# A four-layer diffusion-transformer step: the first gate and up pair by plain block products, and two bursts of the modulation product in other places

## The chip, the cores and the metric

The kernel runs on one core of one Trainium2 chip. The time is the device time of one execution in microseconds (us), from the first to the last instruction with what lies around them; lower is better. TensorE (PE) does the matrix products, VectorE (DVE) and ScalarE (ACT) the elementwise work, GpSimd (POOL) some of it, and SyncE (SP) issues nearly all transfers.

## The reference

Four layers, each with its own token mixer, run over 640 tokens (512 latent, 128 context) with D = 1024 and a feed-forward width of 2816. All data are float32. What matters here:

```python
for li in range(DEPTH):
    mp = adaln(c_ctx[None, :], w_mod[li], b_mod[li])      # silu(c) @ w_mod + b_mod, 6 vectors of D
    ms = adaln(c, w_mod[li], b_mod[li])
    ...                                                   # mixer: op, os_ (with the output product w_o)
    xp = xp + mp[2] * op
    xs = xs + ms[2] * os_
    xp = xp + mp[5] * swiglu(modulate(rms_norm(xp, norm2_g[li]), mp[3], mp[4]), ffn_w_gate[li], ffn_w_up[li], ffn_w_down[li])
    xs = xs + ms[5] * swiglu(modulate(rms_norm(xs, norm2_g[li]), ms[3], ms[4]), ffn_w_gate[li], ffn_w_up[li], ffn_w_down[li])
# swiglu(h) = (silu(h @ w_gate) * (h @ w_up)) @ w_down
```

## The kernel before

Activations lie transposed: 8 feature blocks of 128 partitions by 640 tokens, and a matrix product works on the token halves 0..319 and 320..639. A float32 product is made of three products of split operands (high by high, high by low, low by high; tiles `hh`, `hl` of the activations and `whi`, `wlo` of the weights). A weight block comes in as `raw` by a transfer that SP issues; ACT casts it to `whi`, and DVE subtracts to get `wlo` (both in `two`).

`rest(L)` is the second part of layer L: the second half of the output product w_o, the residual, the RMS norm's statistics, gate and up, and down. `halves_first` runs the output product; for its last two feature blocks it does token half 0 of both blocks, then token half 1 (24 products each). `stat` squares x on ACT (L494), sums on DVE (`t`, L496) and lets TensorE add over the partitions (the matmuls `big<-t,consts`); ACT makes `rstd` of the result (L505, L512).

Gate and up are 2 x 11 matrices, each of 256 output features by 1024 inputs, numbered m = 0..21 (gate and up in turn; a gate with its up is a pair). Each is computed by the Strassen-Winograd scheme: 7 block products in place of 8 for a 2 x 2 split of weights (A11..A22, output halves by input halves) and activations (B11..B22, input halves by token halves). A block product is 12 matmuls of 128 x 128 by 128 x 320 (4 blocks of 128 inputs, three products each). The scheme needs the sums S1..S4 of the weights (`make_a`, DVE, L695, then cast and split as a weight is) and T1..T4 of the activations (`make_b`), and result sums on DVE (`sv`, L719 and below). `make_b` multiplies by `rstd` (DVE, L656), makes the high part on ACT and the low part on DVE (L649) for B11 and B21 tile by tile, then the T tiles, and B22 last.

The modulation of layer L+1 is computed meanwhile: a **burst** is a transfer of 4 x 512 KB (`rawm`, L455, in `mod_load`) and 16 matmuls (`sm<-rawm,cond`; the trace has 32 rows for them); after every second burst ACT copies the result out (`modev`), and 4 small matmuls (`sm<-consts,modev`) and DVE add it up. `rawm` has room for one burst, so the transfer of a burst waits for the matmuls of the one before. `fill(n)` puts n bursts in at its place in the program; layers 0 to 2 have such bursts, layer 3 has none.

The order on each engine is set by a scheduler that takes the instructions by their priority in the program, except where `issue_after` ties one to another. Each engine goes through its own list in order, and so does SP's queue of transfers. There are 4 slots for `raw`, 9 each for `whi` and `wlo`, 4 for `sum`, and 6 PSUM banks named `big`.

Of the kernel before, what the change touches and what calls it, by code (L numbers as in the profile page):

```python
# [8 lines left out]
F32 = mybir.dt.float32  # L9
F32R = mybir.dt.float32r  # L10
AF = mybir.ActivationFunctionType
ALU = mybir.AluOpType
# [250 lines left out]
class Net:  # L263
# [6 lines left out]
    def mm(self, out, lhsT, rhs, start, stop):  # L270
        return self.nc.tensor.matmul(out, lhsT=lhsT, rhs=rhs, start=start, stop=stop, skip_group_check=True)  # L271
# [205 lines left out]

    def flush(self):
        while self.filler:
            self.fill(1)  # L480
# [144 lines left out]
    def make_b(self, pool, L, B, raws):  # L625
# [36 lines left out]
        for i in range(HALF):  # L662
            for d in (i, i + HALF):
                raw(d, hi)
                p, m = raws[d][:, NL:], more[:, d:d + 1]
                nc.scalar.activation(p, p, AF.Identity, bias=m)
            a, b, t = raws[i], raws[i + HALF], t3[i // 2][:, i % 2]
            self.sub(nc.vector, t, b[:, hi], a[:, hi])
            self.sub(nc.vector, a[:, hi], a[:, hi], a[:, lo])
            two("T1", i, hi, a[:, hi])  # L670
# [9 lines left out]
        for i in range(HALF):  # L680
            two("22", i + HALF, hi, raws[i + HALF][:, hi], shift[:, i + HALF, 0:1])
# [16 lines left out]
    def block(self, out, A, B, start, stop):  # L698

        h, l = self.two(A, self.nc.vector)  # L700
        for k, (xh, xl) in enumerate(B):
# [3 lines left out]
            self.mm(out, l[:, c], xh, False, stop and k == len(B) - 1)  # L705

    def gate_up(self, fp, L, name, i, B, pair):
# [32 lines left out]
        if i == 0:  # L740
            self.block(d, A["S1"], B["T1"], True, True)
        self.block(b, A["S2"], B["T2"], True, True)
        add(v1, b, s1)
        if i:
            self.block(d, A["S1"], B["T1"], True, True)
# [8 lines left out]
        if up:  # L754
            for r in (1, 0):
                hi, lo = (fp.tile([P, T], F32R, tag="a", name=n, bufs=16) for n in ("ah", "al"))
                nc.scalar.copy(hi, pair[r])
                self.sub(nc.vector, lo, pair[r], hi.bitcast(F32))
                pair[r] = (hi, lo)
# [39 lines left out]
    def rest(self, L):  # L799

        nc, tc, a = self.nc, self.tc, self.a
        with tc.tile_pool(name=f"ffn{L}", bufs=1, reuse_waits="tile") as fp:
            self.slots(fp)
            todo = 0
            if L + 1 < self.depth:
                c0 = self.mod_done.get(L + 1, 0)
                todo = (6144 - c0) // (4 * MODW) * (ND // BURST) + 1 - 2 * EDGE
                self.filler = [self.mod_parts(L + 1, c0, 6144, fp)]
            B, raws = {}, {}
# [11 lines left out]
            self.fill(EDGE)  # L821
# [9 lines left out]
            ahead(0)  # L831
            ahead(1)
            next(gens[0])
            next(gens[1])
            next(B_steps)
            for part, (i0, i1) in enumerate(PAIRS):
                if part:
                    ahead(2 * i0)
                for m in range(2 * i0, 2 * i1):
                    if m > 1:  # L840
                        next(gens[m])
                    next(gens[m])
                    if 0 < m < 2 * i1 - 1:
                        ahead(m + 1)
                    next(gens[m])
# [909 lines left out]
```

## Time and profile before

| | |
|---|---|
| runs (median of 3; lowest to highest) | 3220.17 us (3213.5 to 3220.33) |
| the profiled execution's own time | 3216.05 us |
| its span, first to last instruction | 3214.0 us |
| mean granted TensorE clock | 0.976 of full speed |
| TensorE busy, of the span | 94% |
| VectorE / ScalarE / GpSimd busy | 67% / 48% / 19% |

The profiled execution takes 2.05 us beside its span and lies 4.1 us under the median of the runs. TensorE is busy for nearly the whole span, but the granted clock is below full speed in places, and there a matmul counts as busy for longer; and busy shares are means over stages with different limits.

### The profile page before, as it was taken

How to read it: one execution, taken by the hardware profiler on the slowest of the kernel's cores; microseconds unless marked ns; L12 is line 12 of the kernel's file. 1: busy time of each engine (PE TensorE's matmuls, PEld its weight loads, DVE VectorE, ACT ScalarE, POOL GpSimd, SP SyncE). 2: the span in 40 equal slices, each digit the busy share in tenths (PEclk: the TensorE clock that was granted, in tenths of full speed). 3: DMA queues.
4: the chain of work that ended last, by engine and by line, in shares of the span. 5: the costliest groups of instructions: out<-in, count | busy, mean ns of one | idle time of the engine just before them, and what ended most of it. 6: DMA issues, size and time to landing. Idle time of an engine off the chain costs nothing.

```text
span 3214.0 us, 57273 instructions
## 1 busy us (share of the span) xinstructions
PE 3029.7 (94%) x21901; PEld 2841.6 (88%) x21901; DVE 2161.6 (67%) x4522; ACT 1528.5 (48%) x3264; POOL 607.1 (19%) x691
## 2 busy tenths in 40 slices
PE   7998989999999989999986899899999999899999
PEld 6997879999988779999985778899998878799999
DVE  5555587666586768585768766867575775875765
ACT  4555454333356755242446664434243576543432
POOL 2553200000044420000025542000001553100000
PEclk9998999999999999999998999999999999899999
DMA  8346563232433342222211224522233111132322
GB/s 265 97 123 208 176 224 102 70 92 94 147 102 128 112 155 76 83 83 76 87 53 37 63 75 143 170 89 80 83 132 118 52 32 32 53 99 70 96 66 86
DMA packets 159027, 331.41 MB, mean 103 GB/s; under 512 B 18592, under 2 KB 40480, under 8 KB 158752
## 3 DMA queue, kind: packets, MB, share of 16 engines
q1 hardware_dynamic: 155584, 323.46, 32.3%
q8 instruction: 173, 2.83, 0.4%
q10 hardware_dynamic: 3168, 4.28, 0.4%
q14 instruction: 102, 0.84, 0.1%
HBM read 303.86 MB, written 4.28 MB: 96 GB/s over the span
## 4 chain that ended last, share of the span: by engine, by line
PE 81%; DVE 8%; DMA 5%; ACT 3%; issue 1%; POOL 1%; SPq 0%; DVEq 0%; ACTq 0%; POOLq 0%
PE big L271 53%; PE sm L271 18%; PE S L271 6%; PE tp L1009 3%; DMA rawm<-in_wmod 3%; DMA k<-k 1%; PE tp L271 1%; DMA raw<-in_wall 1%; DVE st L1030 1%; ACT p L1031 1%; DVE x L603 1%; DVE wlo L319 1%; ACT pt L285 0%; DVE qs L958 0%; DVE hl L999 0%
## 5 line engine op out<-in xcount | busy, mean ns | idle before, releaser
L271 PE MATMUL big<-hh,whi 128*128 128x320 f32 x2720 | 825.4, 313 | 11.7 <-ACT hh L645 5.6
L271 PE MATMUL big<-hl,whi 128*128 128x320 f32 x2720 | 829.0, 311 | 6.3 <-DVE hl L649 3.6
L271 PE MATMUL big<-hh,wlo 128*128 128x320 f32 x2720 | 821.0, 310 | 0.0
L318 ACT CAST whi<-raw 128x512 fp32r<-128x512 f32 (+2 forms) x636 | 383.3, 607 | 709.2 <-PE big L271 554.0
L271 PEld LDWEIGHTS big<-hh,whi 128*128 128x128 f32 x2720 | 508.8, 190 | 25.8 <-ACT hh L645 7.8
L271 PEld LDWEIGHTS big<-hl,whi 128*128 128x128 f32 x2720 | 510.1, 189 | 12.0 <-DVE hl L649 6.2
L271 PEld LDWEIGHTS big<-hh,wlo 128*128 128x128 f32 x2720 | 508.2, 189 | 0.1
L319 POOL TENSOR_TENSOR wlo<-raw,whi 128x512 fp32r<-128x512 f32 (+2 forms) x148 | 196.7, 1342 | 1634.0 <-ACT whi L318 1600.6
L319 DVE TENSOR_TENSOR wlo<-raw,whi 128x512 fp32r<-128x512 f32 (+1 forms) x488 | 325.1, 670 | 142.1 <-ACT whi L318 136.1
L318 ACT CAST whi<-sum 128x512 fp32r<-128x512 f32 x352 | 217.6, 619 | 300.1 <-PE big L271 264.6
L271 PE MATMUL big<-ah,wlo 128*128 128x320 f32 x1408 | 329.1, 309 | 0.0
L271 PE MATMUL big<-ah,whi 128*128 128x320 f32 x1408 | 329.0, 310 | 0.0
L271 PE MATMUL big<-al,whi 128*128 128x320 f32 x1408 | 328.6, 309 | 0.0
L319 DVE TENSOR_TENSOR wlo<-sum,whi 128x512 fp32r<-128x512 f32 x352 | 240.8, 684 | 54.5 <-ACT whi L318 52.9
L1041 POOL TENSOR_SCALAR p<-p,st 128x640 f32<-128x640 f32 (+2 forms) x256 | 197.7, 778 | 285.2 <-DVE st L1040 172.0
L603 DVE SCALAR_TENSOR_TENSOR x<-big,mod,x 128x128 f32<-128x128 f32 (+2 forms) x384 | 146.2, 432 | 150.7 <-PE big L271 150.3
L271 PEld LDWEIGHTS big<-ah,whi 128*128 128x128 f32 x1408 | 237.3, 188 | 1.3 <-issue 0.8
L271 PEld LDWEIGHTS big<-al,whi 128*128 128x128 f32 x1408 | 237.3, 188 | 0.3
L271 PEld LDWEIGHTS big<-ah,wlo 128*128 128x128 f32 x1408 | 237.3, 188 | 0.2
L271 PE MATMUL sm<-whi,hh 128*128 128x256 f32 (+1 forms) x770 | 225.1, 297 | 1.7 <-DVE qs L287 1.1
L271 PE MATMUL sm<-wlo,hh 128*128 128x256 f32 (+1 forms) x770 | 223.3, 292 | 0.2 <-POOL wlo L319 0.2
L271 PE MATMUL sm<-whi,hl 128*128 128x256 f32 (+1 forms) x770 | 223.1, 291 | 0.0
(260 smaller groups left out, 5419.3 us busy)
## 6 DMA issues: line engine op xcount, KB each, us to landing
raw<-in_wall SPq DMA_DIRECT2D x676, 256.0 KB, 2.6
rawm<-in_wmod SPq DMA_DIRECT2D x176, 512.0 KB, 5.8
k<-k SPq DMA_DIRECT2D x38, 384.0 KB, 4.2
bias<-in_nabias SPq DMA_DIRECT2D x16, 576.0 KB, 7.2
raw<-in_wmod SPq DMA_DIRECT2D x32, 256.0 KB, 5.7
qpe<-pes SPq DMA_DIRECT2D x56, 80.0 KB, 2.1
raw<-in_wall SPq DMA_DIRECT2D x32, 128.0 KB, 2.1
out_y<-x ACTq DMA_DIRECT2D x8, 320.0 KB, 2.2
```

Of the source, the lines that this page charges most:

```text
L271: return self.nc.tensor.matmul(out, lhsT=lhsT, rhs=rhs, start=start, stop=stop, skip_group_check=True)
L318: self.nc.scalar.copy(hi, raw)
L319: eng.tensor_tensor(lo, raw, hi.bitcast(F32), ALU.subtract)
L603: self.last = self.nc.vector.scalar_tensor_tensor(xs, halves[b][:, p0:p1], self.mcol(L, i, d, c), xs, ALU.mult, ALU.add)
L1009: self.nc.tensor.transpose(out, in_, self.net.ident)
L1030: nc.vector.tensor_reduce(nm, s, axis=AX.XY, op=ALU.max, negate=True)
L1031: nc.scalar.activation(p.rearrange("p (a b) -> p a b", a=2), s, AF.Exp, bias=nm, accum_out=den)
L1041: nc.gpsimd.tensor_scalar(p, p, rd, 1.0, ALU.mult, ALU.mult)
```

## The change

The first pair of each layer is computed by plain block products (`first_pair`), 8 for its gate and 8 for its up in place of 7 each (192 matmuls for the pair instead of 168), token half 0 first (B11 and B21), then token half 1 (B12 and B22). It needs no S sums, no T tiles and no result sums, but the tiles of B12, for which `make_b` has 4 new pairs of tiles (named `h12`); `make_b` makes B12 and B22 in a step of their own ahead of the T tiles. The first burst's load is put into the program ahead of the output product; its matmuls come after the output product's last matmul, and those of the second burst between the token halves of the first pair (`fill_here`). One burst fewer is spread over the 22 matrices.

```diff
     def mm(self, out, lhsT, rhs, start, stop):
-        return self.nc.tensor.matmul(out, lhsT=lhsT, rhs=rhs, start=start, stop=stop, skip_group_check=True)
+        self.last_mm = self.nc.tensor.matmul(out, lhsT=lhsT, rhs=rhs, start=start, stop=stop, skip_group_check=True)
+        return self.last_mm
...
+    def fill_here(self):
+
+        with self.tc.issue_after(self.last_mm.ins):
+            self.fill(1)
...
                 raw(d, hi)
                 p, m = raws[d][:, NL:], more[:, d:d + 1]
                 nc.scalar.activation(p, p, AF.Identity, bias=m)
+            x12 = pool.tile([P, 2, 320], F32R, tag="a", name="h12", bufs=16)
+            slots.append([x12[:, j:j + 1].rearrange("p a b -> p (a b)") for j in range(2)])
+            two("12", len(slots) - 1, slice(0, 320), raws[i][:, hi], shift[:, i, 0:1])
+            two("22", i + HALF, hi, raws[i + HALF][:, hi], shift[:, i + HALF, 0:1])
+        yield
+        for i in range(HALF):
...
-        for i in range(HALF):
-            two("22", i + HALF, hi, raws[i + HALF][:, hi], shift[:, i + HALF, 0:1])
         yield
...
+    def first_pair(self, fp, L, B, pair):
+
+
+        nc = self.nc
+        W = {}
+        for name in ("gate", "up"):
+            for r, f in enumerate((0, NF // 2)):
+                for n in range(2):
+                    raw = self.slot("raw")
+                    nc.sync.dma_start(raw, self.a["wall"][WIDX[L, name, f][0] + n])
+                    W[name, r, n] = self.two(raw, nc.vector)
+        pair.extend(fp.tile([P, T], F32, tag="t", name="y", bufs=4) for _ in range(2))
+        for c in range(2):
+            for name in ("gate", "up"):
+                for r in range(2):
+                    out, y = self.ps("big")[:, :320], pair[r][:, 320 * c:320 * c + 320]
+                    for n in range(2):
+                        h, l = W[name, r, n]
+                        for k, (xh, xl) in enumerate(B[f"{n + 1}{c + 1}"]):
+                            w = slice(k * P, (k + 1) * P)
+                            self.mm(out, h[:, w], xh, n == 0 and k == 0, False)
+                            self.mm(out, h[:, w], xl, False, False)
+                            self.mm(out, l[:, w], xh, False, n == 1 and k == HALF - 1)
+                    if name == "gate":
+                        self.silu = nc.scalar.activation(y, out, AF.Silu)
+                    else:
+                        nc.vector.tensor_tensor(y, y, out, ALU.mult)
+            yield
+        self.pair_parts(fp, pair)
+        yield
...
-                todo = (6144 - c0) // (4 * MODW) * (ND // BURST) + 1 - 2 * EDGE
+                todo = (6144 - c0) // (4 * MODW) * (ND // BURST) - 2 * EDGE
                 self.filler = [self.mod_parts(L + 1, c0, 6144, fp)]
+                self.fill(1)
...
-            self.fill(EDGE)
+            self.fill_here()
...
-            ahead(0)
-            ahead(1)
-            next(gens[0])
-            next(gens[1])
+            first = self.first_pair(fp, L, B, pairs[0])
+            next(first)
             next(B_steps)
+            self.fill_here()
+            next(first)
+            next(B_steps)
+            next(first)
```

**TensorE around the statistics of layer 0.** These rows stand on TensorE at the end of token half 0 of the output product's last blocks, before:

```order
L271 MATMUL big<-hl,whi 128x320
L271 MATMUL big<-hh,wlo 128x320
L271 MATMUL sm<-rawm,cond 32x256 x16
L271 MATMUL big<-t,consts 128x320
L271 MATMUL big<-hh,whi 128x320
L271 MATMUL big<-hl,whi 128x320
```

and now:

```order
L271 MATMUL big<-hl,whi 128x320
L271 MATMUL big<-hh,wlo 128x320
L271 MATMUL big<-t,consts 128x320
L271 MATMUL big<-hh,whi 128x320
L271 MATMUL big<-hl,whi 128x320
```

The burst that stood between the output product and the first statistics' matmul is gone from there. Some 20 matmuls further on, at the end of token half 1, the rows before are:

```order
L271 MATMUL big<-hl,whi 128x320
L271 MATMUL big<-hh,wlo 128x320
L271 MATMUL sm<-rawm,cond 32x256 x16
L271 MATMUL big<-t,consts 128x320 x2
L271 MATMUL big<-hh,whi 128x320 x2
L271 MATMUL sm<-consts,modev 128x8 x2
L271 MATMUL big<-hl,whi 128x320
```

and now:

```order
L271 MATMUL big<-hl,whi 128x320
L271 MATMUL big<-hh,wlo 128x320
L271 MATMUL big<-t,consts 128x320 x2
L271 MATMUL sm<-rawm,cond 32x256 x16
L271 MATMUL big<-hh,whi 128x320 x4
L271 MATMUL big<-hl,whi 128x320
L271 MATMUL big<-hh,wlo 128x320
```

The burst ahead of the second statistics' matmuls is gone too, and one burst now stands behind them, ahead of the first matmul of gate and up. The next burst stands 96 matmuls later, between the token halves; before, four bursts stood within about 110 matmuls behind the second statistics.

**VectorE in layer 0, where token half 1 of the activations is made.** `h_5328` to `h_5355` are the tiles of B12, `hl` beside them those of B22, and L743 is the multiplication of up's result (of PSUM) by gate's. Now (none of the L655 rows that write `h_...` is there before):

```order
L655 SCALAR_TENSOR_TENSOR hl<-raw,mod,hh 128x320
L655 SCALAR_TENSOR_TENSOR h_5328<-raw,mod,h_5328 128x320
L662 TENSOR_TENSOR raw<-raw,rstd 128x320 x2
L655 SCALAR_TENSOR_TENSOR hl<-raw,mod,hh 128x320
L655 SCALAR_TENSOR_TENSOR h_5337<-raw,mod,h_5337 128x320
L662 TENSOR_TENSOR raw<-raw,rstd 128x320 x2
L655 SCALAR_TENSOR_TENSOR hl<-raw,mod,hh 128x320
L743 TENSOR_TENSOR y<-y,big 128x320
L655 SCALAR_TENSOR_TENSOR h_5346<-raw,mod,h_5346 128x320
L662 TENSOR_TENSOR raw<-raw,rstd 128x320 x2
L655 SCALAR_TENSOR_TENSOR hl<-raw,mod,hh 128x320
L614 TENSOR_TENSOR raw<-raw 128x320 x5
L655 SCALAR_TENSOR_TENSOR h_5355<-raw,mod,h_5355 128x320
```

The multiplication, which has to wait for TensorE, stands ahead of the third and fourth of the four B12 tiles and of the last two of the B22 tiles, with five subtractions for the T tiles (L614) between them. Before, the first multiplication of up's result (L729) stood among T tiles:

```order
L608 TENSOR_TENSOR raw<-raw 128x320
L649 SCALAR_TENSOR_TENSOR hl<-raw,mod,hh 128x320
L608 TENSOR_TENSOR raw<-raw 128x320 x2
L319 TENSOR_TENSOR wlo<-sum,whi 128x512
L673 TENSOR_TENSOR raw<-raw 128x320
L729 TENSOR_TENSOR y<-y,big 128x320
L608 TENSOR_TENSOR raw<-raw 128x320
L649 SCALAR_TENSOR_TENSOR hl<-raw,more,hh 128x320
L649 SCALAR_TENSOR_TENSOR hl<-raw,mod,hh 128x320
```

**SP's queue in layer 0, from the last bursts of the output product on.** Before (L691 loads weight blocks for gate and up, L308 others, L455 bursts):

```order
L308 DMA raw<-in_wall 128x512 x3
L455 DMA rawm<-in_wmod 128x1024 x4
L691 DMA raw<-in_wall 128x512 x7
L455 DMA rawm<-in_wmod 128x1024 x4
L691 DMA raw<-in_wall 128x512
L455 DMA rawm<-in_wmod 128x1024 x4
L691 DMA raw<-in_wall 128x512 x3
L455 DMA rawm<-in_wmod 128x1024 x12
L691 DMA raw<-in_wall 128x512
L455 DMA rawm<-in_wmod 128x1024 x4
L691 DMA raw<-in_wall 128x512 x7
L455 DMA rawm<-in_wmod 128x1024 x4
```

and now (L726 loads the first pair's weight blocks, L701 those of later matrices, L456 bursts):

```order
L309 DMA raw<-in_wall 128x512 x3
L456 DMA rawm<-in_wmod 128x1024 x4
L726 DMA raw<-in_wall 128x512 x8
L701 DMA raw<-in_wall 128x512 x6
L456 DMA rawm<-in_wmod 128x1024 x8
L701 DMA raw<-in_wall 128x512 x5
L456 DMA rawm<-in_wmod 128x1024 x4
L701 DMA raw<-in_wall 128x512 x4
L456 DMA rawm<-in_wmod 128x1024 x4
L701 DMA raw<-in_wall 128x512 x8
L456 DMA rawm<-in_wmod 128x1024 x4
```

The transfer of the first burst stands at the same place in both. The next one, which stood behind 7 weight blocks, now stands behind 14, and a further one directly behind it, with 5 blocks after it.

## Rows read from the trace of the kernel before

**Rows 1.** Engines over the span (page, part 1).

```profile
PE 3029.7 (94%) x21901; PEld 2841.6 (88%) x21901; DVE 2161.6 (67%) x4522; ACT 1528.5 (48%) x3264; POOL 607.1 (19%) x691
```

**Rows 2.** The chain that ended last, whole span: start us, us, what.

```profile
417.03 7.89 DMA rawm<-in_wmod
428.42 6.49 DMA rawm<-in_wmod
...
476.26 298.72 PE big L271 x2036
```

**Rows 3.** Windows, layers 0, 1, 2, 3, then steady gate and up.

```profile
core 0: us, PE busy (x) PEld busy (x) DVE busy (x) ACT busy (x) POOL busy (x), PEclk, DMA share, GB/s
405.50:417.80 12.30, 9.65 (x98) 6.90 (x97) 8.66 (x22) 7.51 (x18) 4.12 (x4) 1.00 0.61 202
417.80:476.30 58.50, 50.09 (x407) 42.33 (x406) 52.06 (x113) 33.32 (x70) 0.00 (x0) 0.94 0.64 229
1174.30:1183.00 8.70, 6.91 (x65) 5.33 (x68) 5.04 (x14) 5.66 (x15) 1.45 (x2) 1.00 0.74 271
1183.00:1220.30 37.30, 28.11 (x217) 22.34 (x213) 32.91 (x78) 23.72 (x51) 0.00 (x0) 0.91 0.39 138
1982.30:1994.60 12.30, 9.64 (x98) 6.90 (x97) 8.68 (x22) 7.52 (x18) 4.12 (x4) 1.00 0.61 205
1994.60:2057.10 62.50, 51.62 (x407) 42.69 (x405) 52.14 (x113) 33.52 (x70) 0.00 (x0) 0.92 0.62 213
2754.70:2768.00 13.30, 8.63 (x34) 7.05 (x33) 7.86 (x20) 7.33 (x17) 3.11 (x3) 0.74 0.06 21
2768.00:2806.00 38.00, 27.93 (x151) 25.26 (x151) 36.64 (x80) 25.17 (x52) 0.00 (x0) 0.87 0.15 43
774.00:834.00 60.00, 60.00 (x468) 56.64 (x466) 43.05 (x80) 26.92 (x50) 0.00 (x0) 1.00 0.51 172
```

**Rows 4.** TensorE by line, 417.8 to 476.3, layer 0.

```profile
L271 PE MATMUL sm<-rawm,cond 128*32 128x256 f32 x160 | 12.1, 453 | 7.7 <-DMA rawm<-in_wmod 7.7
L271 PE MATMUL sm<-consts,modev 128*128 128x8 f32 x12 | 1.5, 235 | 0.0
```

**Rows 5.** TensorE waits, 2768 to 2806, layer 3.

```profile
PE big L271 <- ACT hh L645: 4.4, 1, 4.4
PE big L271 <- DVE hl L649: 2.0, 4, 1.1
```

**Rows 6.** TensorE timeline, layer 0: start us, us, what, idle before.

```profile
405.58 1.94 PE L271 MATMUL sm<-rawm,cond 128*32 128x256 f32 x32
410.16 0.81 PE L271 MATMUL big<-t,consts 128*128 128x320 f32 x2 [2.65 <-DVE t L496]
...
414.96 1.93 PE L271 MATMUL sm<-rawm,cond 128*32 128x256 f32 x32
416.83 1.08 PE L271 MATMUL big<-t,consts 128*128 128x320 f32 x3
```

**Rows 7.** TensorE timeline, layer 3, behind the first statistics.

```profile
2758.35 1.43 PE L271 MATMUL big<-t,consts 128*128 128x320 f32 x2 [3.58 <-DVE t L496]
...
2760.11 0.47 PE L271 MATMUL big<-hh,wlo 128*128 128x320 f32 x1
2760.38 0.47 PE L271 MATMUL big<-hh,whi 128*128 128x320 f32 x1
...
2763.58 0.31 PE L271 MATMUL big<-hh,whi 128*128 128x320 f32 x1
```

**Rows 8.** VectorE by line, 2768 to 2806, layer 3.

```profile
L649 DVE SCALAR_TENSOR_TENSOR hl<-raw,mod,hh 128x320 fp32r<-128x320 f32 x16 | 8.7, 541 | 0.0
...
L319 DVE TENSOR_TENSOR wlo<-sum,whi 128x512 fp32r<-128x512 f32 x5 | 3.4, 679 | 0.0
...
L695 DVE TENSOR_TENSOR sum<-raw 128x512 f32<-128x512 f32 x3 | 2.1, 686 | 0.3 <-DMA raw<-in_wall 0.3
...
L719 DVE TENSOR_TENSOR sv<-big,sv 128x320 f32<-128x320 f32 x4 | 1.9, 482 | 0.0
```

More of the change, by code (lines that the diff above doesn't have):

```diff
@@ L705, in block, with pair_parts @@
             self.mm(out, l[:, c], xh, False, stop and k == len(B) - 1)
+    def first_pair(self, fp, L, B, pair):
[26 more added lines that the diff above has]
+        yield
+    def pair_parts(self, fp, pair):
+        for r in (1, 0):
+            hi, lo = (fp.tile([P, T], F32R, tag="a", name=n, bufs=16) for n in ("ah", "al"))
+            self.nc.scalar.copy(hi, pair[r])
+            self.sub(self.nc.vector, lo, pair[r], hi.bitcast(F32))
+            pair[r] = (hi, lo)
     def gate_up(self, fp, L, name, i, B, pair):
@@ L739, in gate_up @@
         yield
-        if i == 0:
-            self.block(d, A["S1"], B["T1"], True, True)
         self.block(b, A["S2"], B["T2"], True, True)
         add(v1, b, s1)
-        if i:
-            self.block(d, A["S1"], B["T1"], True, True)
+        self.block(d, A["S1"], B["T1"], True, True)
         self.block(b, A["S3"], B["T3"], False, True)
@@ L754, in gate_up @@
         if up:
[L755 to L759, printed above, removed]
+            self.pair_parts(fp, pair)
         yield
@@ L841, in rest @@
                         next(gens[m])
-                    next(gens[m])
+                        next(gens[m])
                     if 0 < m < 2 * i1 - 1:
                         ahead(m + 1)
-                    next(gens[m])
+                    if m > 1:
+                        next(gens[m])
                     while done < todo * (m + 1) // len(mats):
```

## The prediction

> **What bounds the kernel now.** I began with the page. TensorE is busy for 94% of the span [rows 1], so time can come only from its idle stretches, from its clock, or from its work. The chain that ended last has one long piece in each layer's gate and up that is TensorE alone: 2036 matmuls in 298.72 us, 146.7 ns each [rows 2]. A window within it (774 to 834 us) is busy for all of its 60 us at full clock with three bursts in it [rows 3], so a burst in steady gate and up costs its work and no wait. From the start of one burst to what follows it in the timeline are 1.87 us [rows 6]; the small `modev` matmuls take 1.5 us for 12 [rows 4].
>
> What is lost lies at the passage from the output product to gate and up, and the windows of [rows 3] measure it. I split each passage at the first matmul of gate and up, price TensorE's own work at those pitches, and call the rest lost. Layer 0, statistics: 12.30 us for 34 matmuls and two bursts (34 x 0.1467 + 3.74 = 8.7), lost 3.6. Behind them: 58.50 us for 235 matmuls, five bursts and 12 `modev` (34.5 + 9.35 + 1.5 = 45.3), lost 13.2. Layer 1: 8.70 us for 33 matmuls and one burst (6.7), lost 2.0; then 37.30 us for 113 matmuls, three bursts and 8 `modev` (16.6 + 5.6 + 1.0 = 23.2), lost 14.1. Layer 2 has layer 0's counts: lost 3.6, and 62.50 - 45.3 = 17.2. Layer 3, without bursts: 13.30 us for 34 matmuls (5.0), lost 8.3, and 38.00 us for 151 (22.2), lost 15.8. Behind the statistics that is 60.3 us in all.
>
> The reasons differ. In layers 0 to 2 the chain goes through transfers: the bursts stand so close that each waits for its `rawm`, which can't start before the burst ahead is done, 6.5 to 7.9 us each [rows 2], and TensorE stood for 7.7 us for it in layer 0 [rows 4]. In layer 3 VectorE is busy for 36.64 of 38.00 us [rows 3], and TensorE waits for activation tiles, 4.4 us for one of them and 2.0 for others [rows 5]. Both leave TensorE at a lower granted clock: 0.94, 0.91, 0.92 and 0.87 [rows 3], which at two levels, full and half, is (1 - clock) x length = 3.5, 3.4, 5.0 and 4.9 us of the losses above.
>
> **The change part by part.** *More matmuls.* 24 more in each layer at 146.7 ns are 3.5 us, 14.1 in all; this is certain work on the engine that sets the end. The Trainium skill (TensorE: Matmul & The Clock Gate, Back-to-back issue gap) gives the gap of an isolated matmul at the full clock as the column count over 2.4 plus 2.5 ns, which is 135.8 ns for 320 columns and would make it 13.0 us; the trace's pitch is longer, and the sum goes by the trace.
>
> *Less on VectorE.* Per layer the first pair loses 8 sums, 8 low parts of sums and a net 10 result operations and gains 2 low parts and 4 tiles of B12: by the durations of [rows 8], 8 x 0.686 + 8 x 0.679 + 10 x 0.482 - 2 x 0.679 - 4 x 0.541 = 12.2 us busy less. In layer 3's stretch that would leave VectorE near 24.4 us beside 25.7 of TensorE's work, so it no longer sets the pace. Plain products also need only B11 and B21 for the first 96 matmuls: each tile of them feeds 12 (1.76 us) and costs VectorE about 1 us (a multiplication and a low part, 0.48 + 0.54 as operations of their size in [rows 8]). After the first tile TensorE isn't starved.
>
> *Bursts moved.* One burst goes between the token halves, the others come later, where [rows 3] shows that they are free. Their waits for transfers, and the loads queued on SP, go with them: between burst 1 and burst 2 lie 96 matmuls, 14.1 us, against at most 7.9 us for the transfer. The third burst's load now stands ahead of five weight blocks on SP and waits for burst 2. Those blocks serve the fourth matrix, which comes 96 + 84 matmuls behind burst 2, 26 us; I cost this at nothing because that work covers it. If it were gone, the blocks would come late by a transfer, some 8 us in each of three layers. The first burst's load stands where it stood, and the first burst never waited [rows 6]: nothing.
>
> *Cover taken away.* The bursts that filled the two gaps of the statistics are gone from there. In layer 0 TensorE was done at 405.6 and the first statistics came at 410.16 after a burst of 1.94 and 2.65 idle [rows 6]. That end is set by VectorE, so it stays, and the gap is now all idle. The second gap (414.96 to 416.83) also is idle, and burst 1 runs behind it: it starts no later than 416.83 and ends near 418.7, 0.9 us after gate and up began before. One burst fewer is done by then, so 1.9 + 0.9 = 2.8 us are owed in layers 0 and 2. In layer 1, which had only one burst there, it is at most a burst, 1.9. Layer 3 changes nothing there. Together 7.5 us; the bounds are 2.7 (only the 0.9 per layer) and 11.2 (two bursts in each of three layers).
>
> *The clock.* It is the term that no row of before can settle: nothing to lose if TensorE runs through, all of the 16.8 us if the low clock stays. Layer 3 shows what an idle gap does: after 3.58 us without work the matmuls come at 267 ns until 2763.5 and then at 147 [rows 7], about 2.3 us lost. The emptier gaps of layers 0 and 2 are 4.6 us long, so I expect such a stretch there, and keep half of the loss in each layer: 1.75, 1.7, 2.5, 2.45, together 8.4.
>
> The sum: losses 60.3, less 14.1 for matmuls, less 7.5 owed, less 8.4 of clock, is 30.3 us gained (layer 0: 5.2; 1: 7.0; 2: 8.4; 3: 9.9, with roundings). The profiled execution took 3216.05 us, which gives 3185.8. The median of the runs is 4.1 above it, so on their scale I say 3189.
>
> **The rivals.** *Full recovery.* No half clock beyond the old, nothing late: 60.3 - 14.1 - 7.5 = 38.7, 3177 in the profile's scale, up to 3182 on the runs'. For it speaks that gate and up start with 14 us of work that asks little; against it the longer idle gaps.
>
> *VectorE's order gives half of it back.* The multiplication of up's result stands ahead of the third and fourth B12 tiles and the last B22 tiles, and waits for the third of the four output blocks, some 75 of the first 96 matmuls. Behind it come 5.0 us of operations until the last B12 tile (two multiplications and five subtractions at 0.48, three low parts at 0.54); TensorE wants that tile after 21 matmuls, a burst and 9 more, 6.3 us, and in layer 3, without the burst, 4.4. The T tiles come behind those. If the B12 tiles and the T tiles each come 2 us late, 4 us a layer, 16 are lost: 3205. The Trainium skill says that VectorE's queue is a strict FIFO (TensorE: Matmul & The Clock Gate, Architectural detail). So nothing could pass the waiting multiplication; no row here shows it passing.
>
> *Slower: the half clock lasts through the first token half.* If the emptied gaps throttle TensorE and the starting tiles come too thinly to raise it again, 96 matmuls at 267 instead of 147 ns cost 11.5 us a layer, 46 in all. With the 8.4 counted once that is 38 above the forecast, 3227. It decides from some 80 of the 96 matmuls on in every layer: below that the change still gains. For it speaks that the clock fell in each layer already; against it that in layer 3 it rose again after 5 us of work [rows 7]. The Trainium skill has the throttled state as the default and activity as what releases it (same page, Part 1: The HAM clock gate), and by that rule dense products raise it, as the trace agrees (267 ns, then 147).
>
> *No difference.* The freed time is taken by another wait, such as SP's queue behind the third burst: three layers of 8 us and some of VectorE's, 3216 to 3220.
>
> **How the numbers follow.** A measurement of this kernel can tell 0.2%, 6.4 us, from no change. Forecast (3183 to 3197) 0.58; full recovery 0.14; half given back 0.15, of which 0.04 ends within 0.2%; no difference 0.04; slower 0.09. So faster 0.83, same 0.08, slower 0.09. The range goes from 3174, full recovery with the lower bound of what is owed, to 3212, the far end of half given back; outside lie the slower case, no difference and the tails of the others.
>
> **What the changed profile would show.** Right: the idle time before `sm<-rawm,cond` at these passages falls from 7 to 10 us to almost none; the stretch behind the statistics holds gapless matmuls; the granted clock over the passages rises to 0.96 or more; 96 more matmuls; 4.6 us idle before the first `big<-t,consts` of layers 0 and 2. Wrong: TensorE waiting for L743's engine, for the B12 tiles or for T tiles by more than 2 us a layer; matmuls at 267 ns behind burst 1; weight blocks landing late behind the third burst; or a lower clock elsewhere in gate and up, which no row here would have told.

## The result and the profile after

The changed kernel takes 3162.05 us (median of 4 runs, 3156.47 to 3165.95) where the kernel before takes 3216.84 on the same chip (4 runs): a ratio of 0.9829, 95% interval 0.9807 to 0.985. That is 54.8 us gained, where 30.3 were forecast, and below the range's lower end of 3174. The profiled execution took 3162.51 us, 53.5 less than that of before.

The page of the changed kernel, the line that answers to [rows 1], and the shares of its chain:

```profile
PE 3018.2 (95%) x21997; PEld 2843.3 (90%) x21997; DVE 2116.7 (67%) x4442; ACT 1517.4 (48%) x3248; POOL 611.8 (19%) x691
...
PE 37%; DVE 2%; ACT 1%; POOL 1%; DMA 1%; issue 1%; DVEq 0%; ACTq 0%; SPq 0%; POOLq 0%
```

TensorE is busy for 95% in place of 94%. The chain can't be compared with that of before as a whole: followed back from the end, it breaks off at 1827 us, and its shares sum to 43%. From the end of token half 0 in layer 2 to the end of the program, where both traces have it, transfers of bursts hold 2.9% of the chain before and 0.6% after. The windows of the four passages, each from the output product's token half 0 to the first matmul of gate and up, and the 50 us behind it (38 in layer 3), answer to [rows 3]:

```profile
core 0: us, PE busy (x) PEld busy (x) DVE busy (x) ACT busy (x) POOL busy (x), PEclk, DMA share, GB/s
407.28:420.16 12.88, 9.70 (x67) 7.30 (x65) 9.60 (x23) 8.23 (x19) 2.06 (x2) 0.87 0.29 85
420.16:470.16 50.00, 50.00 (x382) 47.75 (x379) 42.86 (x92) 31.26 (x66) 0.00 (x0) 1.00 0.45 158
1165.82:1176.32 10.50, 8.18 (x67) 5.82 (x65) 8.75 (x21) 8.07 (x19) 0.87 (x1) 1.00 0.37 106
1176.32:1226.32 50.00, 50.00 (x382) 47.76 (x379) 42.90 (x93) 31.26 (x66) 0.00 (x0) 1.00 0.45 157
1956.57:1966.91 10.34, 8.15 (x67) 5.80 (x65) 8.61 (x21) 7.91 (x19) 1.07 (x2) 1.00 0.37 107
1966.91:2016.91 50.00, 50.00 (x382) 47.76 (x379) 42.83 (x92) 31.24 (x66) 0.00 (x0) 1.00 0.46 158
2715.98:2724.61 8.63, 6.30 (x35) 4.86 (x33) 6.90 (x17) 6.30 (x16) 0.87 (x1) 1.00 0.32 92
2724.61:2762.61 38.00, 37.49 (x253) 36.97 (x252) 35.82 (x79) 27.66 (x60) 0.00 (x0) 1.00 0.07 22
```

Behind the statistics, TensorE is busy for the whole 50 us in layers 0 to 2 and for 37.49 of 38 in layer 3, at a granted clock of 1.00 (before: 0.94, 0.91, 0.92, 0.87). In layers 0 to 2 VectorE is busy for 43 of 50 us, so it runs ahead. The waits for bursts of [rows 4] are gone, and of TensorE's waits in layer 3 [rows 5] 1.6 us are left, from 2724.6 to 2785 us (what is waited for, us in total, times, longest):

```profile
PE big L271 <- ACT whi L319: 1.1, 1, 1.1
PE big L271 <- ACT sv L785: 0.5, 1, 0.5
```

In the TensorE timeline of layer 0 (start, length, what, idle before), which answers to [rows 6],

```profile
409.52 0.89 PE L271 MATMUL big<-t,consts 128*128 128x320 f32 x2 [2.08 <-DVE t L502]
...
417.56 0.81 PE L271 MATMUL big<-t,consts 128*128 128x320 f32 x2 [1.10 <-ACT t L500]
418.29 1.93 PE L271 MATMUL sm<-rawm,cond 128*32 128x256 f32 x32
```

burst 1 stands behind the last statistics' matmul, as the order had it, but the first statistics waited for 2.08 us, not for the 4.6 that I had kept.

To compare many runs I cut every profiled execution into three kinds of stretch by TensorE's timeline: **S** from the end of the output product's token half 0 to the first matmul of gate and up (four together), **F** from there to the first statistics' matmul at the layer's end, or the last matmul (four together), and **A** the rest, which is attention and the output product. **att2** is the part of A from layer 1's last statistics' matmul to layer 2's output product, the stretch in which GpSimd's order will matter. Layer 2 shows the cut, before:

```profile
1626.71:1982.37 355.66, 302.35 (x1971) 259.79 (x1969) 251.92 (x570) 217.86 (x492) 157.08 (x193) 0.94 0.23 63
1982.37:1994.55 12.18, 9.52 (x97) 6.85 (x97) 8.56 (x22) 7.47 (x18) 4.05 (x4) 1.00 0.61 207
1994.55:2452.72 458.17, 447.29 (x3179) 433.88 (x3177) 313.52 (x596) 181.08 (x333) 1.30 (x1) 0.99 0.36 116
```

and after:

```profile
1607.50:1956.57 349.07, 299.35 (x1971) 259.11 (x1970) 252.55 (x575) 218.29 (x493) 162.32 (x194) 0.95 0.24 66
1956.57:1966.91 10.34, 8.15 (x67) 5.80 (x65) 8.61 (x21) 7.91 (x19) 1.07 (x2) 1.00 0.37 107
1966.91:2413.67 446.76, 446.76 (x3236) 435.70 (x3232) 300.93 (x574) 177.54 (x327) 2.60 (x2) 1.00 0.38 121
```

The 355.66, 12.18 and 458.17 us of A, S and F became 349.07, 10.34 and 446.76. For all runs (us; the ratio is to the kernel before, measured beside it):

| kernel | S | F | A | att2 | median | ratio, 95% interval |
|---|---|---|---|---|---|---|
| before | 49.1 | 1795.2 | 1365.7 | 321.5 | 3216.84 | |
| changed | 42.4 | 1756.8 | 1357.6 | 315.4 | 3162.05 | 0.9829, 0.9807 to 0.985 |
| changed_again | 42.4 | 1756.8 | 1360.3 | 315.4 | 3169.36 | 0.9849, 0.9822 to 0.9876 |
| plain_only | 47.9 | 1754.4 | 1363.0 | 320.8 | 3172.09 | 0.9863, 0.9848 to 0.9878 |
| bursts_only | 52.1 | 1789.2 | 1357.2 | 316.9 | 3214.11 | 0.9983, 0.9971 to 0.9995 |
| sums_late | 41.7 | 1812.6 | 1369.9 | 324.2 | 3226.81 | 1.0032, 1.0019 to 1.0044 |
| sums_dummy | 60.0 | 1756.8 | 1355.6 | 315.9 | 3187.04 | 0.9902, 0.9885 to 0.9919 |
| burst_in_gap | 38.2 | 1756.3 | 1372.8 | 322.1 | 3174.24 | 0.9857, 0.9832 to 0.9883 |
| lo_on_pool | 50.5 | 1757.1 | 1364.4 | 317.3 | 3177.61 | 0.9869, 0.9846 to 0.9892 |
| gate_plain | 53.0 | 1761.9 | 1369.4 | 320.4 | 3189.86 | 0.9912, 0.9887 to 0.9936 |
| gap_layer0 | 40.0 | 1757.4 | 1372.8 | 327.1 | 3174.75 | 0.9873, 0.9857 to 0.989 |
| gap_layer1 | 40.4 | 1756.2 | 1355.8 | 312.0 | 3159.27 | 0.9829, 0.9814 to 0.9844 |
| gap_layer2 | 41.8 | 1756.5 | 1357.5 | 315.4 | 3164.37 | 0.9843, 0.9828 to 0.9857 |
| gap_layers12 | 39.4 | 1755.7 | 1357.3 | 313.4 | 3158.62 | 0.9813, 0.98 to 0.9827 |

F, S and A of the changed kernel are 38.4, 6.7 and 8.1 us shorter than before, 53.2 together. By layer, S was 12.2, 11.4, 12.2 and 13.4 us and is 12.9, 10.5, 10.3 and 8.6. These stretches don't hold the same work: in layers 0 to 2 two bursts stand in S before and one after, so three bursts, 5.6 us, moved from S to F. The forecast, in the same parts, was F 32.2 shorter, S 1.9 longer (its 7.5 owed, less the 5.6) and A the same.

### The profile page after: what moved, and what is told of

Its sections match the earlier page's. It is cut to its first block, busy times and chain, and to the rows that moved or that the text cites. A ratio compares the mean times of both kernels' runs of the same rounds, so it can differ in the third digit from the quotient of the medians.

```text
span 3160.7 us, 57340 instructions
## 1 busy us (share of the span) xinstructions
PE 3018.2 (95%) x21997; PEld 2843.3 (90%) x21997; DVE 2116.7 (67%) x4442; ACT 1517.4 (48%) x3248; POOL 611.8 (19%) x691
## 5 line engine op out<-in xcount | busy, mean ns | idle before, releaser
L271 PE MATMUL big<-hl,whi 128*128 128x320 f32 x2688 | 814.7, 309 | 1.7 <-DVE hl L1045 1.7
L271 PE MATMUL big<-hh,whi 128*128 128x320 f32 x2688 | 811.2, 311 | 1.7 <-ACT whi L319 1.1
L271 PE MATMUL big<-hh,wlo 128*128 128x320 f32 x2688 | 807.7, 310 | 0.0
L320 POOL TENSOR_TENSOR wlo<-raw,whi 128x512 fp32r<-128x512 f32 (+2 forms) x148 | 207.1, 1414 | 1593.0 <-ACT whi L319 1559.6
L271 PEld LDWEIGHTS big<-hh,whi 128*128 128x128 f32 x2688 | 499.1, 188 | 12.2 <-issue 4.5
L271 PEld LDWEIGHTS big<-hl,whi 128*128 128x128 f32 x2688 | 501.5, 188 | 3.4 <-DVE hl L1045 2.8
L271 PEld LDWEIGHTS big<-hh,wlo 128*128 128x128 f32 x2688 | 499.2, 188 | 0.3
L319 ACT CAST whi<-sum 128x512 fp32r<-128x512 f32 x320 | 197.0, 619 | 281.3 <-PE big L271 240.6
L320 DVE TENSOR_TENSOR wlo<-sum,whi 128x512 fp32r<-128x512 f32 x320 | 218.6, 685 | 45.8 <-ACT whi L319 43.1
```

Of the source, the lines that this page charges most:

```text
L271: self.last_mm = self.nc.tensor.matmul(out, lhsT=lhsT, rhs=rhs, start=start, stop=stop, skip_group_check=True)
L319: self.nc.scalar.copy(hi, raw)
L320: eng.tensor_tensor(lo, raw, hi.bitcast(F32), ALU.subtract)
```

## The experiments

**The two halves of the change, each alone.** First the plain pair with the bursts put in as before:

```diff
-                todo = (6144 - c0) // (4 * MODW) * (ND // BURST) - 2 * EDGE
+                todo = (6144 - c0) // (4 * MODW) * (ND // BURST) + 1 - 2 * EDGE
                 self.filler = [self.mod_parts(L + 1, c0, 6144, fp)]
-                self.fill(1)
...
-            self.fill_here()
+            self.fill(EDGE)
...
             next(B_steps)
-            self.fill_here()
             next(first)
```

> The plain first pair alone: the bursts' loads and matmuls are put in as before the change (two steps of the filler behind the output product, one more spread over the matrices). Theory A (the lighter work of VectorE is what pays, ahead of the statistics and behind them): layers 0 to 3 all gain, total within 5 us of the changed kernel, 3157 to 3167 us; the first gap of the statistics is shorter than before and filled by a burst. Theory B (in layers 0 to 2 the spacing of the bursts is what pays): only layer 3 gains, some 14 us, total 3198 to 3206.

Then the bursts moved, with the first pair by seven block products:

```diff
...
-                todo = (6144 - c0) // (4 * MODW) * (ND // BURST) + 1 - 2 * EDGE
+                todo = (6144 - c0) // (4 * MODW) * (ND // BURST) - 2 * EDGE
                 self.filler = [self.mod_parts(L + 1, c0, 6144, fp)]
+                self.fill(1)
...
-            self.fill(EDGE)
+            self.fill_here()
...
             next(gens[1])
+            self.fill_here()
             next(B_steps)
```

> The bursts moved as in the change (load ahead of the output product, first burst behind it, second burst behind the first four block products), the first pair by seven block products as before. Theory A: VectorE sets the pace at the start of gate and up as it does in layer 3 of the kernel before, and the sums still delay the statistics, so 0 to 10 us gained, 3207 to 3217 us; layer 3 as before. Theory B: layers 0 to 2 gain some 35 us, 3178 to 3186.

The plain pair alone has a ratio of 0.9863, and its F is 40.8 us shorter than before, in all four layers; the bursts alone have 0.9983, some 5 us, with F 6.0 shorter and S 3.0 longer. Theory B falls. Theory A's size was off too: 3172.09 lies above its 3157 to 3167. Whether the bursts' new places add anything to the plain pair isn't shown, since the interval of plain_only meets those of the changed kernel's two rows. With the bursts moved alone, TensorE waits in layer 0, in the 60 us behind the statistics, for other things than `rawm` (in layers 1 and 2 waits of 2.1 and 0.8 us for it are left):

```profile
PE big L271 <- ACT hh L651: 2.5, 1, 2.5
PE big L271 <- ACT sv L742: 1.0, 1, 1.0
PE big L271 <- ACT hh L654: 1.0, 2, 0.9
PE big L271 <- DVE sv L725: 0.6, 1, 0.6
PE big L271 <- DVE hl L614: 0.4, 1, 0.4
```

Those are the high and low parts of the activations and the result sums, with VectorE busy for 53.30 of 60 us. ScalarE, which most of these waits name, itself waits there for VectorE's results, 14.5 us in all; the two longest are shown (engine, tile and line, then what is waited for):

```profile
421.28:481.28 60.00, 54.41 (x425) 48.06 (x422) 53.30 (x115) 33.84 (x70) 0.00 (x0) 0.97 0.65 227
...
ACT whi L319 <- DVE sum L701: 3.8, 2, 2.6
ACT hh L654 <- DVE raw L679: 3.6, 4, 1.7
```

So in the kernel before, the bursts stood in the very places where TensorE would otherwise have waited for VectorE. The trace named the transfer as what ended the wait, and that was true of the instruction, but behind it stood VectorE. In the run with the plain pair alone the next burst stands behind both token halves, without a line of the bursts' code changed, and TensorE waits for nothing in the 50 us behind the statistics of layers 0 to 2.

**The sums ahead of the statistics.** In the kernel before, the sums of the first gate and up are tied behind the residual:

```diff
             raw[n] = self.slot("sum")
-            nc.vector.tensor_tensor(raw[n], raw[x], raw[y], op)
+            with contextlib.ExitStack() as st:
+                if i == 0:
+                    st.enter_context(self.tc.issue_after(self.last.ins))
+                nc.vector.tensor_tensor(raw[n], raw[x], raw[y], op)
```

> The kernel before, with the sums S1 to S4 of the first gate and up (8 operations of VectorE) tied behind the residual of the output product. If these sums and what hangs on them delay the statistics, the time from the output product's token half 0 to the first statistics' matmul falls from 4.6, 1.9, 4.6, 3.7 us (layers 0 to 3) to 1.3 to 2.5. Rival (the gap shrank for another reason): it stays as it was. The total is open: VectorE has the same work, only later, so 3210 to 3225 us.

And in the changed kernel, eight additions are put back whose results nobody reads:

```diff
                     nc.sync.dma_start(raw, self.a["wall"][WIDX[L, name, f][0] + n])
+                    nc.vector.tensor_tensor(self.slot("sum"), raw, raw, ALU.add)
                     W[name, r, n] = self.two(raw, nc.vector)
```

> The changed kernel with 8 additions of 128 x 512 on VectorE put beside the first pair's weight blocks, results unused: the work of the 8 sums that the change removed. If the removed sums are what shortened the statistics' gap, it goes back to 3.5 to 4.6 us in layers 0, 2 and 3 and the total rises by 6 to 12 us to 3168 to 3174; the granted clock falls at the start of the first pair only if the idle gap is what lowers it. Rival (the gap is shorter because bursts no longer stand in it, or the low parts are fewer): the total stays within 3 us of the changed kernel.

Here VectorE adds each weight block to itself. The time from token half 0 to the first statistics' matmul, layers 0 to 3, was 4.6, 1.9, 4.6, 3.7 us before, 2.2, 1.4, 1.3, 1.4 in the changed kernel, 1.9, 1.9, 1.9, 0.4 with the sums late (a burst fills it in layers 0 to 2) and 4.4, 4.5, 4.2, 4.8 with the dummies. S went down by 7.4 us in the one, with the bursts where they were before, and up by 17.6 in the other, and with the dummies F is that of the changed kernel. With the sums late F is 17.4 us longer than before, so the whole is slower (3226.81, a ratio of 1.0032): VectorE has the same work, and behind the statistics TensorE waits for it longer. VectorE's groups in layer 0, from the start of the output product's second part to the first statistics, before,

```profile
L603 DVE SCALAR_TENSOR_TENSOR x<-big,mod,x 128x320 f32<-128x320 f32 (+2 forms) x20 | 7.8, 439 | 0.0
L319 DVE TENSOR_TENSOR wlo<-raw,whi 128x512 fp32r<-128x512 f32 x8 | 5.2, 684 | 0.6 <-ACT whi L318 0.5
...
L695 DVE TENSOR_TENSOR sum<-raw 128x512 f32<-128x512 f32 x3 | 2.0, 682 | 7.0 <-DMA raw<-in_wall 7.0
L319 DVE TENSOR_TENSOR wlo<-sum,whi 128x512 fp32r<-128x512 f32 x3 | 2.0, 677 | 0.0
L695 DVE TENSOR_TENSOR sum<-sum,raw 128x512 f32<-128x512 f32 x1 | 1.1, 1096 | 0.0
```

and after:

```profile
L609 DVE SCALAR_TENSOR_TENSOR x<-big,mod,x 128x320 f32<-128x320 f32 (+2 forms) x20 | 7.8, 441 | 0.0
L320 DVE TENSOR_TENSOR wlo<-raw,whi 128x512 fp32r<-128x512 f32 x11 | 7.3, 683 | 6.2 <-ACT whi L319 6.1
...
L705 DVE TENSOR_TENSOR sum<-raw 128x512 f32<-128x512 f32 x1 | 0.7, 721 | 0.6 <-DMA raw<-in_wall 0.6
```

Sums and low parts took 2.0 + 1.1 + 2.0 + 5.2 = 10.3 us before and take 7.3 + 0.7 = 8.0 after, with the residuals `x` and the squares' sums in the same queue. The 2.3 us between them are about what the gap lost in layer 0 (4.6 to 2.2). The long waits in both, 7.0 us for a weight block and 6.1 for its cast, lie early and are of one size, so they are not what went. The gaps moved as expected in both, though layer 3's fell below what was given with the sums late (0.4), and layer 1's rose with the dummies far above what it had been before (4.5 against 1.9). The totals were missed: 3226.81 where 3210 to 3225 was given, and the dummies cost 15.8 us of span between the profiled executions, and 17 to 24 by the ratios of the table, where 6 to 12 was given. A dummy also reads its weight block and so may hold the block's slot for longer; that wasn't separated from its time on VectorE.

**How much of the pair has to be plain, and whose low parts.** Only the gate by plain products, its up by seven:

```diff
-        for name in ("gate", "up"):
+        for name in ("gate",):
...
             self.fill_here()
+            ahead(1)
             next(first)
+            next(gens[1])
             next(B_steps)
-            next(first)
...
```

> Only the gate of the first pair by plain products, its up by seven block products: 12 matmuls fewer a layer than the changed kernel (1.76 us, 7 in all), but the T tiles and one matrix's sums are wanted some 10 us earlier. Theory A (VectorE's tiles set the pace): TensorE waits for T tiles again, 4 to 8 us a layer, and the low clock with it, so 3170 to 3185. Rival (96 plain matmuls are cover enough): 3153 to 3158.

And half of the low parts on GpSimd:

```diff
-                    W[name, r, n] = self.two(raw, nc.vector)
+                    W[name, r, n] = self.two(raw, (nc.vector, nc.gpsimd)[n])
```

> The changed kernel with half of the first pair's low parts (4 of 8 per layer) on GpSimd in place of VectorE. If work of VectorE ahead of the statistics still sets their time, the stretch from the output product's token half 0 to gate and up falls by another 1 to 2 us a layer, 3154 to 3159. Rival (the rest of the gap is the chain residual, square, sum itself): no change, 3160 to 3164; if GpSimd's operations (1.3 us each) come late for the first pair, up to 3170.

With the gate alone, 3189.86, above the 3170 to 3185 of theory A: F is 5.1 us longer although 48 matmuls (7.0 us) are gone, 4.1 of it in layer 3, but the larger losses are in A (1369.4, 9.1 more than in the second profile of the changed kernel) and in S (53.0 against 42.4), where sums of up stand ahead of the statistics again. TensorE waits there in layer 0 as it did with the dummies:

```profile
PE big L271 <- DVE t L502: 4.8, 1, 4.8
```

So the direction of theory A held, but the place I had named for it, the T tiles, took only the smaller part. Layer 3 doesn't fit: sums stand ahead of its statistics too, and its S is 8.1 us against 8.6, so the amount of VectorE's work alone doesn't give the time of the statistics.

The low parts on GpSimd made it worse, S 50.5, against my expectation; 3177.61 is above all that was given (3170 at most) and 8.3 above the changed kernel measured beside it. Three low parts left VectorE ahead of the statistics of layer 0, yet in layers 0 and 2 the statistics came 2.8 and 3.2 us later (in layers 1 and 3 they did not), and in layer 0 VectorE stood longer at the one sum left:

```profile
L320 DVE TENSOR_TENSOR wlo<-raw,whi 128x512 fp32r<-128x512 f32 x8 | 5.3, 695 | 6.4 <-ACT whi L319 6.4
...
L705 DVE TENSOR_TENSOR sum<-raw 128x512 f32<-128x512 f32 x1 | 0.7, 692 | 3.5 <-DMA raw<-in_wall 3.5
```

That is 3.5 us against 0.6 in the changed kernel, and what stands behind the sum in VectorE's queue waits with it. GpSimd takes longer for a low part (1.48 us for each of the three, where VectorE takes 0.70), and a weight block's slot is free only when that is done, which would delay the block that the sum waits for; that chain was not tried by itself.

**A burst back in the gap, and attention.** The first burst ahead of the first statistics:

```diff
             def after_wo(b, d):
+                if b == (0,) and d == ND - 1:
+                    self.fill_here()
                 self.stat(fp, d, b)
...
-            self.fill_here()
             done = 0
```

> The changed kernel with the first burst's matmuls put back behind the output product's token half 0, ahead of the first statistics (layers 0 to 2). If an empty gap there is what the change costs (the prediction's cover taken away), the burst fits in 1.4 to 2.2 us of idle time and 3 to 6 us are gained, 3156 to 3159. Rival (the gap has shrunk below a burst's 1.9 us and the burst now delays the statistics): within 2 us of the changed kernel, or above it.

> The changed kernel unaltered, profiled a second time. Theory C (the 6 us by which the attention stages were shorter in its first profile are chance, the phase of the clock, not the change): the stages from the residual's last statistics to the next output product differ from the first profile by several us in all, while gate, up and down repeat to 0.3 us a layer (446.8, 431.2, 446.8, 432.1). Rival (the change made attention faster): attention repeats at 381.6, 264.0, 315.4, 266.9 us to within 1. Median 3158 to 3166.

S, with one burst in each of layers 0 to 2 as in the changed kernel, fell by 4.2 us as the first theory has it, but the median is not below that of the changed kernel measured beside it (3174.24 and 3169.36): A is 12.5 us longer than in the second profile of the changed kernel, 6.7 of it in att2. In the second profile of the changed kernel F repeated to 0.01 us a layer and att2 at 315.4, while A of layers 0 and 1 moved by 1 to 4 us and the median, 3169.36, lay above the 3158 to 3166 given. So there is chance, and neither theory C nor its rival holds in every layer; but layer 2's attention, in these two profiles, shows none. Nothing in attention's code differs between these kernels. What differs is the order that the scheduler gave its instructions: an edit in one layer can change it in later ones. GpSimd's rows at one place of layer 2's attention, from the built program (`p` is a softmax multiplication, `sqh<-ktok` squares for the norm of keys), before:

```
TENSOR_TENSOR sqh<-ktok 128x256
TENSOR_SCALAR p<-p,st 128x640
TENSOR_TENSOR sqh<-ktok 128x256
TENSOR_SCALAR p<-p,st 128x640
TENSOR_TENSOR sqh<-ktok 128x256
```

and in the changed kernel:

```
TENSOR_TENSOR sqh<-ktok 128x256
TENSOR_TENSOR sqh<-ktok 128x256
TENSOR_TENSOR sqh<-ktok 128x256
TENSOR_TENSOR sqh<-ktok 128x256
TENSOR_SCALAR p<-p,st 128x640
```

There are two such places. Kernels with the changed order in both (changed, changed_again, sums_dummy, bursts_only, lo_on_pool; the last two differ a little further on) took 315.4 to 317.3 us for att2, with one of them other 320.4 to 322.1 (before, plain_only, burst_in_gap, gate_plain), with both other 324.2 (sums_late). Three runs tested that with the burst in the gap in one layer alone, each with an order known ahead; for layer 0:

```diff
             def after_wo(b, d):
+                if L == 0 and b == (0,) and d == ND - 1:
+                    self.fill_here()
                 self.stat(fp, d, b)
...
-            self.fill_here()
+            if not (L == 0):
+                self.fill_here()
```

> The changed kernel with the first burst back ahead of the first statistics in layer 0 alone. What is tested is attention, which the change doesn't touch: by the built order, GpSimd's instructions in layer 2's attention now stand as in the kernel before in one place and as in the plain pair alone in another, and in layer 1's as in the run with the burst in the gap. Theory D (the scheduler's order there is what attention's time follows; kernels with the changed kernel's order took 315.4 to 316.9 us in layer 2, with one of the two places other 320.4 to 322.1, with both 324.2): layer 2's attention 323 to 325 us, layer 1's 267 to 269. Theory C (chance, the clock's phase): anything from 315 to 322. Statistics of layer 0: 10.1 us in place of 12.9. Median 3 to 12 us above the changed kernel by D.

> The same in layer 1 alone: everything up to there is built as in the changed kernel, and layer 2's attention has an order of its own on GpSimd (places 358 to 407), seen in no run so far. Theory D: layers 0 and 1 have the changed kernel's attention times (380 to 382 and 264 to 266 us), layer 2's differs from 315.4 by more than 1 us in either direction and repeats no clock phase; statistics of layer 1 9.7 us in place of 10.5. Theory C: layer 2 between 315 and 322.

> The same in layer 2 alone; GpSimd's order is the changed kernel's everywhere. Theory D: attention of layers 1 and 2 as in the changed kernel, 264 to 266 and 315.4 us to within 0.5; statistics of layer 2 9.7 us in place of 10.3; median within 3 us of the changed kernel, and the best of all if anything. Theory C: layer 2's attention 315 to 322.

Layer 2's attention, in windows of the runs with the burst in the gap of layer 0, 1 and 2 (one row each, of three traces):

```profile
1616.38:1943.51 327.13, 276.57 (x1759) 233.79 (x1757) 229.46 (x529) 204.50 (x466) 142.11 (x181) 0.91 0.21 54
```

```profile
1614.41:1926.43 312.02, 266.24 (x1759) 226.37 (x1757) 230.89 (x529) 202.82 (x466) 143.89 (x181) 0.95 0.22 57
```

```profile
1616.87:1932.28 315.41, 266.87 (x1760) 227.79 (x1758) 231.44 (x529) 203.52 (x466) 144.90 (x181) 0.94 0.22 56
```

The order with both places other took 327.1 us, the order of its own 312.0, the changed order 315.41. Theory D holds in layer 2, with 2 us more than expected in the first: its order of GpSimd is that of sums_late, which took 324.2, so one order can differ by 2.9 us, and still the groups don't overlap. For layers 0 and 1 it was off by up to 0.9 us (379.1 where 380 to 382 were expected, 266.5 where 267 to 269 were), which is no more than two profiles of one kernel differ there. In the first the granted clock is 0.91 against 0.94 to 0.95, so part of the longer time is TensorE at its lower clock; whether the order brings that about is open. That all engines' orders differ between these kernels, not GpSimd's alone, leaves open which engine's order counts.

**The best of them.** Layers 1 and 2 together:

> The changed kernel with the first burst ahead of the first statistics in layers 1 and 2, the two where that shortened the statistics without a longer attention. GpSimd's order is that of the run with layer 1 alone. Theory D: attention of layer 2 repeats 312.0 us to within 1, statistics of layers 1 and 2 are 9.7 us each (10.5 and 10.3 in the changed kernel), so 4 to 5 us below the changed kernel where clock and chip agree: a ratio of 0.980 to 0.983 to the kernel before. Theory C: layer 2's attention somewhere in 315 to 322 and no gain over the changed kernel.

The ratio is 0.9813 (0.98 to 0.9827), the lowest of all; S of layers 1 and 2 was 9.7 each, and att2 was 313.4, 0.4 outside what theory D had allowed. Its interval meets those of the changed kernel, so that it is better than the changed kernel isn't shown.

## Why the prediction was wrong

**Right.** The loss was where [rows 3] had it, and the plain pair removed it: F fell by 38.4 us, by 7.3, 9.9, 11.4 and 9.9 in layers 0 to 3, with 14.1 us of matmuls and 5.6 of bursts added to it, so some 58 of the 60.3 us lost came back. 24 matmuls a layer cost their time, VectorE's saving took it off the path, and the bursts, once in steady gate and up, cost their work alone. None of the waits that I had feared there came: not for the multiplication of L743, not for weight blocks behind the third burst, and the slower rival's half clock didn't last into the first token half in any layer.

**Wrong: "That end is set by VectorE, so it stays, and the gap is now all idle", and with it "Layer 3 changes nothing there."** This is the failed step. VectorE did set that end, but I had counted VectorE's saving only behind the statistics. Sums and their low parts stood ahead of them too, and the change took away most of these, though it put low parts of plain blocks there. The gap from token half 0 to the first statistics, to stay at 4.6 us in layers 0 and 2, fell to 2.2 and 1.3. In layer 3, which has no bursts, it fell from 3.7 to 1.4, the granted clock of the window rose from 0.74 [rows 3] to 1.00, and S is 4.7 us shorter. For all layers I had 1.9 us more in S, and measured 6.7 less; sums_late and sums_dummy show the cause from both sides.

**Right in its sign, too large: "cover taken away".** In layers 0 to 2 S is 2.1 us shorter with 5.6 us less work in it, so 3.5 us are owed there, net of what the shorter gaps gave back, where I had put 7.5. The burst put back into the gap shows that cover still has a price, 4.2 us of S for the same number of bursts. The longer S of the plain pair alone (47.9) says nothing against that, since it holds one more burst in each of layers 0 to 2. S of layer 0 in plain_only and in burst_in_gap:

```profile
408.01:420.87 12.86, 10.43 (x102) 7.37 (x101) 9.75 (x23) 7.62 (x18) 2.01 (x2) 1.00 0.73 242
409.27:419.37 10.10, 9.03 (x70) 6.41 (x69) 7.89 (x20) 6.79 (x16) 2.04 (x2) 1.00 0.82 283
```

The row of layer 1 was also misread. Its window was cut at 1183.00, but the first matmul of gate and up came at 1185.68, behind a second burst, so before the change layer 1 too had two bursts in S and not "only one":

```profile
1182.87 1.93 PE L271 MATMUL sm<-rawm,cond 128*32 128x256 f32 x32 [1.79 <-DMA rawm<-in_wmod]
1184.74 1.34 PE L271 MATMUL big<-t,consts 128*128 128x320 f32 x4
1185.68 0.70 PE L271 MATMUL big<-hh,whi 128*128 128x320 f32 x2
```

**Wrong: "keep half of the loss in each layer" for the clock.** 8.4 us were put down as still lost, and the clock behind the statistics was 1.00 in all four layers. sums_dummy shows that this doesn't hang on short gaps: with 4.2 to 4.6 us of waiting and a clock of 0.79 in S of layer 0 it was 1.00 again in the first pair:

```profile
404.42:420.35 15.93, 10.61 (x66) 8.02 (x64) 11.67 (x27) 9.10 (x20) 5.95 (x5) 0.79 0.30 84
420.35:470.35 50.00, 50.00 (x382) 47.75 (x379) 42.85 (x92) 31.24 (x66) 0.00 (x0) 1.00 0.45 158
```

The low clock of [rows 3] belonged to the waits inside the passage, and went with them. The Trainium skill says that activity releases the throttle (TensorE: Matmul & The Clock Gate, Part 1: The HAM clock gate); these rows agree. The forecast without this term would have had F 40.6 us shorter; 1.6 of the 2.2 that are missing are the waits left in layer 3, and beside these the layers differ by 0.4 to 1.2 us either way, which I can't place.

**Not in the prediction: A, 8.1 us.** Of these 6.1 lie in layer 2's attention, where the time follows the scheduler's order in repeated runs. The rest is of the size by which two profiles of the changed kernel differ (1357.6 and 1360.3) and is left as chance.

**Right in its amount, wrong in its reason: "In layers 0 to 2 the chain goes through transfers."** The bursts' waits stood where VectorE would have been waited for; moving the bursts alone gained 5 us.

The sum of misses is F 6.2, S 8.6 and A 8.1, 22.9 of the 22.9 us between 53.2 and 30.3. The range's lower end, 3174, doesn't come out of its own terms: full recovery with 2.7 owed is 43.5 us, 3172.6 in the profile's scale and 3176.7 on the runs'. The measured time is below each.

## What to carry to other kernels

When work leaves an engine, price it at every place where that engine is waited for, ahead of the edit too: here an eighth of the gain (6.7 of 53.2 us) lay in an earlier stage whose end I had copied from the trace. Where work moves from one stretch to the next, compare the two together, or count what each holds. A filler that waits may only be standing where something else is late; take the filler away in thought, and ask what the engine would wait for then. And where a scheduler orders the program, an edit in one layer can reorder the next: compare the built order of stages that were not edited, and treat a difference there as an edit with a price of its own.

## What was not expected of the hardware

Gate, up and down take the same time to 0.03 us a layer in the changed kernel's two profiles and with the dummies (446.76, 446.76 and 446.77 in layer 0), so such a stretch, once TensorE never waits, repeats far better than the whole kernel, whose runs spread over 10 us. The two profiles differ by 2.7 us in A; where the other runs' spread lies is not shown. And with three low parts fewer ahead of the statistics of layer 0, VectorE waited longer there: 3.5 us at a sum for its weight block, against 0.6.
